# A two-layer token-mixing backbone: branch products among the attention units, pooling as a unit of its own, adaLN rows transposed one step later

## The chip, the cores and the metric

The kernel runs on one core of a Trainium2 chip. The metric is the device time of one execution in microseconds (us), as the median of several. The engines are called PE (matrix products), DVE (elementwise work), ACT (activations, casts, copies), POOL (elementwise work, slower) and SP (which here only issues DMA).

## What is computed

The reference is a network of two layers over 256 latent tokens and 256 context tokens, width 1024, in float32. Each layer is

```python
h = modulate(layer_norm(x), sh1, sc1)             # sh, sc, g: six rows of 1024 from silu(c) @ ada_w
mix = token_mixing(h, hc, lp, need_ctx)           # need_ctx only in the first layer
x = layer_norm(alpha * x + g1 * mix);  x = layer_norm(alpha * x + g2 * mlp(modulate(x, sh2, sc2)))
# token_mixing:
z, xbc, dt, qkv, pool, fnet, gate = split(h @ in_w + in_b)
y = g_ssd * (ssd(xbc, dt, z) @ ssd_out_w) + g_na * (attention(qkv) @ na_out_w) \
  + g_pool * (pool_branch(pool) @ pool_out_w) + g_fnet * (fourier(fnet) @ fnet_out_w)
mix = y @ mix_out_w                               # g = sigmoid(gate), four times 1024 columns
```

The pool branch takes centred window means (windows 2, 4, 8, 16) of the tokens in four groups of 192 columns, subtracts the token, and multiplies each group by a 192 x 192 matrix. The attention has 16 heads; the SSD has four groups. In the first layer all 512 tokens go through everything (`NX = 512`), in the second only the 256 latent tokens go on behind the mixers (`NX = 256`).

## The kernel before

Activations lie transposed, features on partitions and tokens along the row. Each float32 product is made of three products of rounded halves: `hi` is a rounded copy, `lo` the rest. A weight tile of 128 columns (`W`) is loaded by SP (512 KB), rounded by ACT to `whi` (L153) and subtracted by DVE to `wlo` (L154); there are three buffers. One product of a 1024-deep contraction is 24 matmuls (`mm3`, L186: `h_hi,whi`, `h_lo,whi`, `h_hi,wlo` for each of eight slices). An activation is split in the same way by `split_to` (L200 on ACT, L201 on DVE); in the profile these halves are `part`, or `plh` and `pll` in the pool.

A layer goes on like this. `first_products`, then `Driver.run` over thirteen units: `dt_unit`, and four times `ssd_unit` (group g) and two `attn_unit` (two heads each). A unit is a generator; where it yields, the driver puts in work that has come due. An SSD unit ends with squares summed on PE (L668), a power on POOL (L671), its spreading by PE (L675) and the scaled result `yt` on DVE (L679). An attention unit scores two heads (L719, L720 on PE), takes the softmax (DVE L729, L731, L733; ACT L734; DVE L735, L736; the context part is L745 to L754), transposes it on PE (L764, L772), copies it (ACT L765, L774) and multiplies by the values (L797, L802), which gives `oat` (L805).

Behind the units come the four branches in turn, each a `branch_unit` (L818): for each of eight output tiles a gate (24 matmuls from `h`, then ACT's tanh into `gth`, L816) and a branch product (from the split parts). Branch 0 (SSD) writes `mg` (L832), the others multiply and add (L834 on DVE, L835 on POOL). Each gate is emitted one tile ahead. Between branch 1 (attention) and branch 2 (pool) stands the pool stage in straight code: four `pool_tile`, `pool_map` 0, two `pool_tile`, two gates of branch 2, `pool_map` 1. A pool tile is a product of `h` (24 matmuls), window sums on DVE (`pwa`, `pwb`, L854), scaling (L872), subtraction (L874) and a split (`plh`, `pll`). A map is 21 matmuls over three split tiles with small weights (128 x 384), and writes the parts of branch 2 (L888, L889).

The adaLN rows (`ada_steps`) are made bit by bit between other work: a step multiplies 16 times (L295) into `adarows` (copied by ACT, L302), and `ada_flush` transposes them on PE (L315) for DVE to reduce (L317). Rows as they are needed for a gate are made by `rows_of` (L1027 on DVE, L1029 on PE, L1031 on DVE). At the start of the MLP, L370 transposes the normalised tokens, and DVE makes `h_hi` (L377) and `h_lo` (L378).

The order of an engine's instructions comes from a list scheduler: among those that are ready by its reckoning it takes the one emitted first, where weight loads and splits count as emitted 150 places earlier. So emission order is what the code decides, and each engine then works through its own list in order.

Of the kernel before, what the change touches and what calls it, by code (L numbers as in the profile page):

```python
# [10 lines left out]
F32R = mybir.dt.float32r  # L11
# [4 lines left out]
P = 128  # L16
D = 1024
KD = 8
# [11 lines left out]
NG = ((2,2),(2,2))  # L30
# [6 lines left out]
OFF = {256: 16, 512: 0}  # L37
# [36 lines left out]
def hybrid_backbone_kernel(ctx: ExitStack, tc: tile.TileContext, I, out, dbg=None):  # L74
# [21 lines left out]
    def T2(shape, name, dt=F32):  # L96
        return t2p.tile(shape, dt, tag="t2", name=name)
# [61 lines left out]
    def W(src, kt=KD, cols=P, scale=None, ahead=AHEAD, off=0):  # L159


        n = kt * cols
        hi = whl.tile([P, KD * P + 64], F32R, tag="hi", name="whi")[:, off:off + KD * P]
        lo = whl.tile([P, KD * P + 64], F32R, tag="lo", name="wlo")[:, off:off + KD * P]
        with tc.high_priority(offset=ahead):
            st = load_w(src, kt, cols)
            split_w(st[:, 0:n], n, hi[:, 0:n], lo[:, 0:n], scale)
        hi = hi[:, 0:n].rearrange("p (k c) -> p k c", c=cols)
        lo = lo[:, 0:n].rearrange("p (k c) -> p k c", c=cols)
        return lambda x, k: (hi, lo)[x][:, k, :]  # L170
# [111 lines left out]
    def ada_steps(l):  # L282


        steps = len(ADA_ORDER) // 2
        for n in range(steps):
            if (l, n) not in ready:
                ada_load(l, n)
            sts, ahead = ready.pop((l, n))
            ada_flush(l)  # L290
            pa = PS()
            for q in range(4):
                i, kc = q // 2, q % 2
                for k in range(4):
                    pe.matmul(pa[32 * k:32 * k + 32, 0:256], csil[:, 4 * kc + k, 2 - 2 * i:34 - 2 * i], sts[q](k),  # L295
                              start=(q == 0), stop=(q == 3), tile_position=(0, 32 * k))
            if not ahead:
                c = next(((l, m) for m in range(n + 1, steps) if (l, m) not in ready), (l + 1, 0))
                if c[0] < DEPTH:
                    ada_load(*c)  # L300
            rows = T2([P, 256], "adarows")
            act.copy(rows, pa[:, 0:256])  # L302
            open_[l] = (n, rows)
            yield

    open_, ready = {}, {}
    done = [0] * DEPTH

    def ada_flush(l):
        if l not in open_:  # L310
            return
        n, rows = open_.pop(l)
        pt = PS()
        for i in range(2):
            pe.transpose(pt[:, P * i:P * i + P], rows[:, P * i:P * i + P], ident)  # L315
        tmp = S([P, 2, 4], "adat")
        dve.tensor_reduce(tmp, pt[:, 0:256].rearrange("p (i c r) -> p i r c", i=2, c=4)[:, :, 0:4, :], axis=AX.X,  # L317
                          op=ALU.add)
        for j, g in enumerate(ADA_ORDER[2 * n:2 * n + 2]):
            o = _COLS["ada"] + 2 * g  # L320
            dve.tensor_tensor(mods[l][:, 2 * g:2 * g + 2, :], tmp[:, :, 2 * j:2 * j + 2],
                              colst[l][:, o:o + 2].unsqueeze(2).to_broadcast([P, 2, 2]), op=ALU.add)
# [65 lines left out]
    def layer(l, need_ctx, h, ws, load_x, final, prepare=None):  # L388

        NX = 512 if need_ctx else 256  # L390
# [3 lines left out]
        hx = NX / 512.0  # L394
# [111 lines left out]
        yt = {}  # L506
# [176 lines left out]
        oat = {}  # L683
# [128 lines left out]
        def gate(b, m):  # L812

            pg = inproj(M_GATE + 8 * b + m, NX)
            ths[b, m] = T2([P, 512], "gth")[:, 0:NX]
            act.activation(ths[b, m], pg[:, 0:NX], AF.Tanh, bias=col("gate", 8 * b + m), scale=0.5)  # L816

        def branch_unit(b, name, kt, a):  # L818
            if (b, 0) not in ths:
                gate(b, 0)  # L820
                yield "h", hx
            for m in range(KD):
                if m + 1 < KD and (b, m + 1) not in ths:
                    gate(b, m + 1)
                    yield "h", hx
                th = ths.pop((b, m))
                w = W(I[name][l, m], kt, off=OFF[NX])
                py = PM()
                mm3(py[:, 0:NX], w, a, K8[:kt], lambda t, k: t[k])
                if b == 0:  # L830
                    mg[m] = T2([P, 512], "mg")[:, 0:NX]
                    dve.scalar_tensor_tensor(mg[m], th, 1.0, py[:, 0:NX], op0=ALU.add, op1=ALU.mult)  # L832
                else:
                    dve.scalar_tensor_tensor(th, th, 1.0, py[:, 0:NX], op0=ALU.add, op1=ALU.mult)  # L834
                    pool.tensor_tensor(mg[m], mg[m], th, op=ALU.add)  # L835
                yield "h", hx
# [43 lines left out]
        def pool_map(pr_, pd, phl):  # L880
            ab = ([x[0] for x in pd], [x[1] for x in pd])
            for i in range(3):
                m = 3 * pr_ + i
                w = W(I["pool_w"][l, pr_, i], 3, off=OFF[NX])
                ks = [(k, k) for k in ((0, 1), (0, 1, 2), (1, 2))[i]]
                py = PS()
                mm3(py[:, 0:NX], w, ab, ks, lambda t, k: t[k][:, 0:NX])
                act.activation(phl[0][m], py[:, 0:NX], AF.Identity, scale=col("pscale", m))  # L888
                dve.scalar_tensor_tensor(phl[1][m], py[:, 0:NX], col("pscale", m), phl[0][m].bitcast(F32),  # L889
                                         op0=ALU.mult, op1=ALU.subtract)  # L890
# [81 lines left out]
                split_to(fhl[0][m], fhl[1][m], ft[:, 0:NS].rearrange("p s t -> p (s t)"))  # L972

        def parts(k=KD):
            return tuple([T2([P, 512], f"part{x}", F32R)[:, 0:NX] for _ in range(k)] for x in range(2))

        def split_tiles(src):
            a = parts()
            for m in range(KD):
                split_to(a[0][m], a[1][m], src.pop(m)[:, 0:NX])  # L980
            return a
# [3 lines left out]
        dr = Driver()  # L985
        units = [dt_unit(fp[0])]
        for g in range(4):
            units.append(ssd_unit(g, fp[1:] if g == 0 else None))
            units += [attn_unit(2 * g), attn_unit(2 * g + 1)]
        dr.run(units)  # L990
        if dbg:
            dbg("y", l, [yt[m][:, 0:NX] for m in range(KD)])
            dbg("o", l, [oat[m][:, 0:NX] for m in range(KD)])
        if need_ctx:
            layer_cols(l + 1)
        dr.run([branch_unit(0, "ssd_out_w", KD, split_tiles(yt))])
        dr.run([branch_unit(1, "na_out_w", KD, split_tiles(oat))])
        phl = parts(6)
        pds = [[], []]
        for i in range(3):  # L1000
            pool_tile(0, i, pds[0])
        pool_tile(1, 0, pds[1])
        pool_map(0, pds[0], phl)
        pool_tile(1, 1, pds[1])
        pool_tile(1, 2, pds[1])
        for m in range(NG[l][0]):
            gate(2, m)
        pool_map(1, pds[1], phl)
        dr.run([branch_unit(2, "pool_out_w", 6, phl)])
        fourier_load()  # L1010
        fhl = parts(6)
        fourier(fhl)
        dr.run([branch_unit(3, "fnet_out_w", 6, fhl)])


        mhl = parts()
# [150 lines left out]
        for c in range(4):  # L1167
            if c == 3:
                ada(l, 100)
                ada_flush(l)  # L1170
                if need_ctx:
                    ada(l + 1, 4, 4)
                    ada_flush(l + 1)
                g2 = rows_of(5)
            a2 = parts()
            m0 = 0
            if c == 0 and need_ctx:
                ws = ups
                m0 = len(ws)
                pls = [PM(), PM(), PM(), PS(), PS()][:m0]  # L1180
                for sl in (XS, CS):
                    for m in range(m0):
                        mm3(pls[m][:, sl], ws[m], h2, K8, lambda t, k: t[:, k, sl])
                for m in range(m0):
                    up_sink(pls[m], a2, c, m)
            for m in range(m0, KD):
                w = W(I["mlp_up_w"][l, 8 * c + m], off=48 if c == 1 else OFF[NX])
                ps = PM()
                mm3(ps[:, 0:NX], w, h2, K8, lambda t, k: t[:, k, 0:NX])
                up_sink(ps, a2, c, m)  # L1190
                if need_ctx:
                    ada(l + 1, 1, min(4, (8 * c + m) // 4 + 1))
            if c < 3:
                for n in range(2):
                    def sink(ps, t, n=n, c=c):
                        if c == 0:
                            acc[t, n] = T2([P, 512], "macc")
                            dve.tensor_tensor(acc[t, n], ps, db[n], op=ALU.add)
                        else:
                            dve.tensor_tensor(acc[t, n], acc[t, n], ps, op=ALU.add)  # L1200

                    half(lambda kk: I["mlp_down_w"][l, c, n, kk], a2, sink)
# [199 lines left out]
```

## Time and profile before

| | |
|---|---|
| median of 3 runs | 2121.72 us (2121.46 to 2122.72) |
| the profiled execution | 2120.56 us |
| its span | 2118.8 us |
| PE busy | 96% |
| DVE, ACT, POOL busy | 61%, 48%, 12% |
| bytes read from HBM | 293.75 MB |

The profiled execution is a single one, of which the hardware recorded the instructions; the span is from the first to the last instruction recorded. PE is busy almost throughout, so the profile is to be read for the short stretches in which it is not, one by one in the timeline, and for the clock that it was granted (1.00 is full speed).

### The profile page before, as it was taken

To read this page: it belongs to the slowest core of one execution; us is meant where nothing else is said; L and a number is where in the kernel's file an instruction comes from. 1 tells how busy PE (TensorE), PEld (TensorE's weight loads), DVE (VectorE), ACT (ScalarE), POOL (GpSimd) and SP (SyncE) were. 2 spreads that over 40 slices of the span, in tenths; PEclk is the share of its full clock that TensorE was granted. 3 is DMA by queue.
4 is the path that set the end of the run, shared out by engine and by line. 5 is a ranking of instruction groups with operands and counts; after the bars stand their busy time and mean duration, and the time that the engine had idled before them with its cause. 6 is when DMAs were issued, how large, how long until landed. Compare 5 with 4: busy or idle time off the path is not lost. (4 is left out here: it accounts for less than half of the span.)

```text
span 2118.8 us, 31149 instructions
## 1 busy us (share of the span) xinstructions
PE 2043.7 (96%) x12008; PEld 1703.3 (80%) x12008; DVE 1291.9 (61%) x2319; ACT 1019.9 (48%) x1787; POOL 247.6 (12%) x244
## 2 busy tenths in 40 slices
PE   6999999999999999999999999999999999998998
PEld 3777777777888888878888887877887898997997
DVE  4687686864336534475333357788778557566557
ACT  3576575763323323334232233576667545445443
POOL 0001000000001010112011111001000000112112
PEclk8999999999999999999999999999999999999999
DMA  7534243432332531335343333424345466566664
GB/s 287 172 130 161 98 160 100 159 105 81 99 100 82 181 107 54 99 120 179 117 151 92 98 120 120 172 83 150 109 131 165 122 193 207 184 208 210 190 193 142
DMA packets 94467, 298.16 MB, mean 141 GB/s; under 512 B 10928, under 2 KB 18800, under 8 KB 94320
## 3 DMA queue, kind: packets, MB, share of 16 engines
q1 hardware_dynamic: 94320, 296.19, 43.2%
q8 instruction: 94, 1.54, 0.3%
q14 instruction: 53, 0.43, 0.1%
HBM read 293.75 MB, written 2.39 MB: 140 GB/s over the span
## 5 line engine op out<-in xcount | busy, mean ns | idle before, releaser
L154 DVE TENSOR_TENSOR wlo<-st,whi 128x1024 fp32r<-128x1024 f32 (+3 forms) x382 | 477.0, 1250 | 453.2 <-ACT whi L153 434.4
L153 ACT CAST whi<-st 128x1024 fp32r<-128x1024 f32 (+3 forms) x382 | 386.2, 1012 | 713.0 <-PE pm L186 493.4
L186 PE MATMUL pm<-h_hi,whi 128*128 128x512 f32 (+1 forms) x1944 | 678.2, 349 | 3.3 <-DVE qb L698 1.3
L186 PE MATMUL pm<-h_lo,whi 128*128 128x512 f32 (+1 forms) x1944 | 674.0, 347 | 3.0 <-DVE h_lo L378 3.0
L186 PE MATMUL pm<-h_hi,wlo 128*128 128x512 f32 (+1 forms) x1944 | 673.5, 347 | 0.9 <-DVE wlo L154 0.9
L186 PEld LDWEIGHTS pm<-h_hi,whi 128*128 128x128 f32 x1944 | 367.0, 189 | 54.4 <-issue 6.1
L186 PEld LDWEIGHTS pm<-h_hi,wlo 128*128 128x128 f32 x1944 | 366.7, 189 | 50.2 <-issue 4.8
L186 PEld LDWEIGHTS pm<-h_lo,whi 128*128 128x128 f32 x1944 | 367.4, 189 | 49.1 <-DVE h_lo L378 3.2
L195 PE MATMUL pm<-whi,part 128*128 128x512 f32 x784 | 243.4, 390 | 0.1
L186 PE MATMUL pm<-part,whi 128*128 128x512 f32 (+1 forms) x896 | 218.8, 335 | 2.7 <-DVE part L201 1.1
L195 PEld LDWEIGHTS pm<-whi,part 128*128 128x128 f32 x784 | 146.5, 188 | 31.1 <-DVE part L1019 0.5
L186 PEld LDWEIGHTS pm<-part,whi 128*128 128x128 f32 x896 | 152.4, 188 | 22.3 <-DVE part L201 2.0
L195 PE MATMUL pm<-wlo,part 128*128 128x512 f32 x392 | 152.7, 389 | 0.0
L186 PE MATMUL pm<-part,wlo 128*128 128x512 f32 (+1 forms) x448 | 149.4, 334 | 0.5 <-DVE wlo L154 0.5
L1163 POOL TENSOR_TENSOR relu<-relu 128x512 f32<-128x512 f32 (+1 forms) x64 | 86.3, 1349 | 390.6 <-ACT relu L1160 387.0
L835 POOL TENSOR_TENSOR mg<-mg,gth 128x512 f32<-128x512 f32 (+1 forms) x48 | 55.3, 1152 | 525.0 <-DVE gth L834 348.2
L517 DVE SCALAR_TENSOR_TENSOR cacc<-cv,cols,cacc 128x512 f32<-128x512 f32 (+1 forms) x128 | 92.8, 725 | 8.2 <-ACT cacc L515 6.4
L186 PEld LDWEIGHTS pm<-part,wlo 128*128 128x128 f32 x448 | 84.1, 188 | 9.4 <-DVE wlo L154 0.7
L195 PEld LDWEIGHTS pm<-wlo,part 128*128 128x128 f32 x392 | 73.6, 188 | 15.2
L628 POOL TENSOR_TENSOR line<-line 128x512 f32<-128x512 f32 (+1 forms) x32 | 41.3, 1293 | 260.0 <-ACT line L624 219.4
L624 ACT ACTIVATE line<-line,nA 128x128 f32<-128x128 f32 x192 | 61.3, 395 | 12.1 <-DVE line L622 12.0
L834 DVE SCALAR_TENSOR_TENSOR gth<-gth,pm 128x512 f32<-128x512 f32 (+1 forms) x48 | 26.5, 552 | 63.6 <-PE pm L186 63.6
(260 smaller groups left out, 2540.7 us busy)
## 6 DMA issues: line engine op xcount, KB each, us to landing
st<-in_w SPq DMA_DIRECT2D x184, 512.0 KB, 3.6
ad<-ada_w SPq DMA_DIRECT2D x88, 512.0 KB, 6.0
st<-mlp_up_w SPq DMA_DIRECT2D x64, 512.0 KB, 3.6
st<-mlp_down_w SPq DMA_DIRECT2D x64, 512.0 KB, 3.6
bia<-rpb SPq DMA_DIRECT2D x16, 512.0 KB, 4.9
line<-sums SPq DMA_DIRECT2D x32, 256.0 KB, 6.7
st<-ssd_out_w SPq DMA_DIRECT2D x16, 512.0 KB, 3.6
st<-na_out_w SPq DMA_DIRECT2D x16, 512.0 KB, 3.6
```

Of the source, the lines that this page charges most:

```text
L153: act.copy(hi, st)
L154: dve.tensor_tensor(lo, st, hi.bitcast(F32), op=ALU.subtract)
L186: pe.matmul(ps, w(x, kw), rhs(a[y], ka), start=(i == 0 and j == 0), stop=(i == n - 1 and j == 2))
L195: pe.matmul(ps, a[y][k][:, P * t:P * t + P], w(x, i), start=(k == 0 and j == 0), stop=(k == KD - 1 and j == 2))
L517: dve.scalar_tensor_tensor(acc, c[:, 0:ns, k:k + 256], col("convw", 5 * m + k), acc, op0=ALU.mult, op1=ALU.add)
L624: act.activation(ex[:, t], ex[:, t], AF.Exp, bias=nAv[:, t, d, hd:hd + 1])
L628: pool.tensor_tensor(ed[0][:, 0:NT], ed[0][:, 0:NT], ed[1][:, 0:NT], op=ALU.add)
L834: dve.scalar_tensor_tensor(th, th, 1.0, py[:, 0:NX], op0=ALU.add, op1=ALU.mult)
L835: pool.tensor_tensor(mg[m], mg[m], th, op=ALU.add)
L1163: pool.tensor_tensor(r2, r, r, op=ALU.mult)
```

## The change

Four edits go together.

1. `ada_flush(l)` moves from ahead of a step's 16 matmuls to behind them: the rows of the step before are transposed later.
2. Branch 0 is handed to the driver as the last of the units, instead of in a run of its own. Its `split_tiles(yt)` is called when it gets to the first product; until all eight `yt` are there (`ready`), gates are emitted.
3. The pool stage becomes a unit, `pool_unit`, and runs with branch 1: behind it in the list in the first layer (`need_ctx`), ahead of it in the second, where each map is preceded by a yield `"w", 1` that lets branch 1 in.
4. `parts` puts two 256-column parts into one buffer; the weights of the MLP's second chunk get the same offset as the others (48 before).

```diff
             sts, ahead = ready.pop((l, n))
-            ada_flush(l)
             pa = PS()
...
                               start=(q == 0), stop=(q == 3), tile_position=(0, 32 * k))
+            ada_flush(l)
...
-        def branch_unit(b, name, kt, a):
+        def branch_unit(b, name, kt, a, ready=lambda: True):
...
+                if m == 0:
+                    for n in range(2, KD):
+                        if not ready():
+                            gate(b, n)
+                            yield "h", hx
+                    a = a()
...
-            return tuple([T2([P, 512], f"part{x}", F32R)[:, 0:NX] for _ in range(k)] for x in range(2))
+            n = 512 // NX
+            ts = [[T2([P, 512], f"part{x}", F32R) for _ in range(k // n)] for x in range(2)]
+            return tuple([ts[x][i // n][:, NX * (i % n):NX * (i % n) + NX] for i in range(k)] for x in range(2))
...
+        phl = []
+        def pool_unit():
+            phl.extend(parts(6))
+            pds = [[], []]
+            for i in range(3):
+                pool_tile(0, i, pds[0])
+                yield "h", hx
+            pool_tile(1, 0, pds[1])
+            yield "h", hx
+            if not need_ctx:
+                yield "w", 1
+            pool_map(0, pds[0], phl)
+            pool_tile(1, 1, pds[1])
+            yield "h", hx
+            pool_tile(1, 2, pds[1])
+            yield "h", hx
+            if need_ctx:
+                for m in range(NG[l][0]):
+                    gate(2, m)
+            else:
+                yield "w", 1
+            pool_map(1, pds[1], phl)
+        dr.run(units + [branch_unit(0, "ssd_out_w", KD, lambda: split_tiles(yt), lambda: len(yt) == KD)])
...
-        dr.run([branch_unit(0, "ssd_out_w", KD, split_tiles(yt))])
-        dr.run([branch_unit(1, "na_out_w", KD, split_tiles(oat))])
...
+        b1 = branch_unit(1, "na_out_w", KD, lambda: split_tiles(oat))
+        dr.run([b1, pool_unit()] if need_ctx else [pool_unit(), b1])
+        dr.run([branch_unit(2, "pool_out_w", 6, lambda: phl)])
...
-                w = W(I["mlp_up_w"][l, 8 * c + m], off=48 if c == 1 else OFF[NX])
+                w = W(I["mlp_up_w"][l, 8 * c + m], off=OFF[NX])
```

In the rows below, a `...` stands where rows are left out. Line numbers of the changed kernel are 1 to 20 off behind the changed places (L839 to L896 are L832 to L889 of before, L1051 is L1031).

PE at the end of layer 1's mixers, before: from the last score product of the last head (L720) through its softmax's transposes (L764) to branch 0's first product (`part`).

```order
L720 MATMUL psx<-kk_4244,qb_4101 128x256
L186 MATMUL pm<-h_hi,whi 128x512
...
L764 MATMUL psx<-cons,sc 128x128 x2
L186 MATMUL pm<-h_hi,whi 128x512
...
L764 MATMUL psx<-cons,sc 128x128 x6
L772 MATMUL psx<-cons,scc 128x128 x4
L797 MATMUL psx<-PT,vk 64x256 x8
L802 MATMUL psx<-PC,vk 64x256 x4
...
L186 MATMUL pm<-part_4672,whi 128x512
```

The same place after the change, from the transposes of the last but one head.

```order
L764 MATMUL psx<-cons,sc 128x128 x8
L772 MATMUL psx<-cons,scc 128x128 x4
...
L719 MATMUL psx<-kk_4244,qa_4099 128x256
L720 MATMUL psx<-kk_4244,qb_4101 128x256
L764 MATMUL psx<-cons,sc 128x128 x8
L186 MATMUL pm<-part_4695,whi 128x512
L772 MATMUL psx<-cons,scc 128x128 x4
L186 MATMUL pm<-h_hi,whi 128x512
L186 MATMUL pm<-part_4703,whi 128x512
```

The products of `h` that stood behind the last scores are gone from there, and the first branch product has come up between the last head's L764 and L772.

PE at the end of layer 2's mixers, before, from the last two score products.

```order
L719 MATMUL psx<-kk_14135,qa_14063 128x512
L720 MATMUL psx<-kk_14135,qb_14065 128x512
L186 MATMUL pm<-h_lo,whi 128x256
...
L764 MATMUL psx<-cons,sc 128x128 x2
L797 MATMUL psx<-PT,vk 64x256
L764 MATMUL psx<-cons,sc 128x128 x6
L797 MATMUL psx<-PT,vk 64x256 x7
L186 MATMUL pm<-part_14468,whi 128x256
```

The same place now.

```order
L719 MATMUL psx<-kk_14135,qa_14063 128x512
L720 MATMUL psx<-kk_14135,qb_14065 128x512
L675 MATMUL psx<-cons,rs 128x128 x2
L764 MATMUL psx<-cons,sc 128x128 x2
L797 MATMUL psx<-PT,vk 64x256
L186 MATMUL pm<-part_14543,whi 128x256 x2
L764 MATMUL psx<-cons,sc 128x128
L186 MATMUL pm<-part_14547,whi 128x256
```

Here too the products of `h` (17 before) have left the place behind the scores, L675 of the last SSD group has come there, and branch 0's products begin between the two heads' transposes.

DVE in layer 2, before: `part<-oat` are the halves for branch 1's products, `pwa` and `pll` the first and last step of the pool's tiles.

```order
L832 SCALAR_TENSOR_TENSOR mg<-gth,pm 128x256
L154 TENSOR_TENSOR wlo<-st,whi 128x1024
L201 TENSOR_TENSOR part_15036<-oat,part_15028 128x256
...
L201 TENSOR_TENSOR part_15043<-oat,part_15035 128x256
L834 SCALAR_TENSOR_TENSOR gth<-gth,pm 128x256
...
L854 TENSOR_TENSOR pwa<-pu 128x270
...
L201 TENSOR_TENSOR pll<-pl,plh 128x256
```

DVE in layer 2 after the change, at the end of the pool's tiles.

```order
L881 TENSOR_TENSOR pl<-pl,pu 128x256
L896 SCALAR_TENSOR_TENSOR part_15024<-psx,cols,part_15021 128x256
L201 TENSOR_TENSOR pll<-pl,plh 128x256
L201 TENSOR_TENSOR part_15438<-oat,part_15434 128x256 x2
L201 TENSOR_TENSOR part_15439<-oat,part_15435 128x256 x2
L201 TENSOR_TENSOR part_15440<-oat,part_15436 128x256 x2
L201 TENSOR_TENSOR part_15441<-oat,part_15437 128x256 x2
L841 SCALAR_TENSOR_TENSOR gth<-gth,pm 128x256
```

The halves for branch 1 stood ahead of the whole pool; they now stand behind its last `pll`.

DVE at the start of layer 2's MLP, before.

```order
L1072 TENSOR_SCALAR xn<-xt,lnsum 128x1024
L377 CAST h_hi<-htmp 128x2x256
L378 TENSOR_TENSOR h_lo<-htmp,h_hi 128x2x256
L377 CAST h_hi<-htmp 128x2x256
L378 TENSOR_TENSOR h_lo<-htmp,h_hi 128x2x256
```

The same place now; `grow` is the copy of a gate's rows out of PSUM.

```order
L1092 TENSOR_SCALAR xn<-xt,lnsum 128x1024
L377 CAST h_hi<-htmp 128x2x256
L1051 COPY grow<-psx 16x128
L378 TENSOR_TENSOR h_lo<-htmp,h_hi 128x2x256
L377 CAST h_hi<-htmp 128x2x256
L378 TENSOR_TENSOR h_lo<-htmp,h_hi 128x2x256
```

The copy of the gate's rows has moved in between the first `h_hi` and the first `h_lo`.

## Rows read from the trace of the kernel before

**Rows 1.** Profile page: busy time of each engine, its share of the span, instructions.

```profile
PE 2043.7 (96%) x12008; PEld 1703.3 (80%) x12008; DVE 1291.9 (61%) x2319; ACT 1019.9 (48%) x1787; POOL 247.6 (12%) x244
```

**Rows 2.** PE's waits over the run: who, for what; us, times, longest.

```profile
PE psx L764 <- DVE sc L736: 8.2, 10, 1.1
...
PE psx L295 <- ACT PC L774: 1.1, 1, 1.1
```

**Rows 3.** Timeline of PE, end of layer 1's mixers: start, length, instruction, wait before.

```profile
465.16 2.07 PE L675 MATMUL psx<-cons,rs 128*128 128x128 f32 x8 [0.77 <-POOL rs L671]
...
475.84 0.40 PE L186 MATMUL pm<-h_hi,whi 128*128 128x512 f32 x1
...
490.07 0.51 PE L186 MATMUL pm<-part,whi 128*128 128x512 f32 x1 [0.62 <-DVE part L201]
```

**Rows 4.** The same view of DVE and ACT, the last head's softmax in layer 1.

```profile
475.10 0.42 DVE L729 CUSTOM_DVE_ANT_0 sc<-psx,bia 128x256 f32<-128x256 f32 x1 [1.28 <-PE psx L720]
...
477.95 0.48 DVE L736 TENSOR_SCALAR sc<-sc,mx 128x512 f32<-128x512 f32 x1
...
480.08 0.20 ACT L750 ACTIVATION_READ_ACCUMULATOR scc<-psx,mxc 128x1 f32 x1
```

**Rows 5.** Windows: length, PE busy (matmuls), mean granted clock, DMA share, GB/s.

```profile
464.00:469.00 5.00, 4.23 (x19) 0.66 0.93 312
1441.00:1449.00 8.00, 7.51 (x36) 0.57 0.43 132
1664.00:1672.00 8.00, 4.73 (x30) 1.00 0.33 111
1690.00:1710.00 20.00, 20.00 (x179) 1.00 0.65 200
1799.00:1819.00 20.00, 20.00 (x172) 1.00 0.77 249
1150.00:1170.00 20.00, 20.00 (x90) 1.00 0.27 89
```

**Rows 6.** Timeline of PE, end of layer 2's mixers.

```profile
1658.31 0.71 PE L675 MATMUL psx<-cons,rs 128*128 128x128 f32 x4 [0.34 <-POOL rs L671]
...
1662.44 0.28 PE L186 MATMUL pm<-h_lo,whi 128*128 128x256 f32 x1
...
1664.27 0.28 PE L186 MATMUL pm<-h_hi,wlo 128*128 128x256 f32 x1
1665.66 0.41 PE L764 MATMUL psx<-cons,sc 128*128 128x128 f32 x2 [1.12 <-DVE sc L736]
...
1667.64 0.87 PE L764 MATMUL psx<-cons,sc 128*128 128x128 f32 x6 [0.99 <-DVE sc L736]
1668.87 1.94 PE L797 MATMUL psx<-PT,vk 128*64 128x256 f32 x14 [0.35 <-ACT PT L765]
1671.57 0.84 PE L186 MATMUL pm<-part,whi 128*128 128x256 f32 x2 [0.77 <-ACT part L200]
```

**Rows 7.** Timeline of DVE there, the last head's softmax in layer 2.

```profile
1662.18 0.42 DVE L729 CUSTOM_DVE_ANT_0 sc<-psx,bia 128x256 f32<-128x256 f32 x1
...
1665.03 0.49 DVE L736 TENSOR_SCALAR sc<-sc,mx 128x512 f32<-128x512 f32 x1
```

**Rows 8.** Layer 2's pool stage: windows of PE and DVE, and DVE's timeline.

```profile
1754.39:1789.50 35.11, 31.23 (x254) 1.00 0.58 183
...
1754.39:1789.50 35.11, 28.51 (x55) 1.00 0.58 183
...
1759.42 0.43 DVE L854 TENSOR_TENSOR pwa<-pu 128x270 f32<-128x270 f32 x1
...
1785.72 0.42 DVE L201 TENSOR_TENSOR pll<-pl,plh 128x256 fp32r<-128x256 f32 x1 [0.47 <-ACT plh L200]
```

**Rows 9.** Timeline of PE and DVE, start of layer 2's MLP.

```profile
1927.14 3.46 PE L370 MATMUL psx<-cons,xn 128*128 128x128 f32 x15 [0.30 <-DVE xn L1072]
...
1929.59 0.69 DVE L378 TENSOR_TENSOR h_lo<-htmp,h_hi 128x512 fp32r<-128x512 f32 x1
```

More of the change, by code (lines that the diff above doesn't have):

```diff
@@ L989, in layer @@
             units += [attn_unit(2 * g), attn_unit(2 * g + 1)]
[L990 to L993, printed above, removed]
+        phl = []
[21 more added lines that the diff above has]
+        dr.run(units + [branch_unit(0, "ssd_out_w", KD, lambda: split_tiles(yt), lambda: len(yt) == KD)])
         if need_ctx:
             layer_cols(l + 1)
-        dr.run([branch_unit(0, "ssd_out_w", KD, split_tiles(yt))])
-        dr.run([branch_unit(1, "na_out_w", KD, split_tiles(oat))])
[L998 to L1009, printed above, removed]
+        b1 = branch_unit(1, "na_out_w", KD, lambda: split_tiles(oat))
+        dr.run([b1, pool_unit()] if need_ctx else [pool_unit(), b1])
+        dr.run([branch_unit(2, "pool_out_w", 6, lambda: phl)])
         fourier_load()
@@ L1012, in layer @@
         fourier(fhl)
-        dr.run([branch_unit(3, "fnet_out_w", 6, fhl)])
+        dr.run([branch_unit(3, "fnet_out_w", 6, lambda: fhl)])
         mhl = parts()
```

## The prediction, made before the changed kernel had run

> **What bounds the kernel now.** I read the page first: TensorE (PE) is busy for 96% of the span, VectorE (DVE) for 61% [rows 1]. So only a pause of PE, a slower clock of PE or a slower step from one matmul to the next is worth time. Next the table of PE's waits, which says what is left: its longest group over the run is the attention transposes (L764) waiting for the softmax's last scaling (L736), ten times, 8.2 us, none over 1.1; another is L295 waiting once, 1.1, for a copy of ACT [rows 2]. Then the timelines of the places that the change touches, which give each wait its moment, and windows for the clock. In the rows below a wait in brackets stands behind the instruction that waited. The loss is a little more than the bracket, because the matmuls no longer overlap: the product at 1664.27 would have been followed 0.11 later, at 1664.38; the next starts at 1665.66 [rows 6], which is 1.28 for a bracket of 1.12. I add 0.2 to 0.3 to a bracket.
>
> **The change part by part**, as gain or loss of PE time.
>
> (a) adaLN rows one step later. Over the run nothing is computed twice or left out; the transposes L315 go behind the sixteen L295 of the next step. The one place where this changes what PE waits for is early in layer 1, where L295 stood behind L315 and waited 1.1 [rows 2]: that goes if the copy is ready 2 us later. Elsewhere the transposes stand between products that cover them. +1.1, bounds 0 and +1.1.
>
> (b) Branch 0 among the last units of layer 1. What goes: the wait of L675 for the normalisation on GpSimd (0.77) and that of the first branch product for its split on DVE (0.62) [rows 3], with the overlap 1.7. [...] The change puts a gate's 24 products ahead of L675, so that L668's result has 5.4 us to come back (24 at 0.227, since 20 us hold about 88 of this layer's [rows 5]), and I let the fall go too. Together +3.4.
>
> What comes: the order rows show that the change emits three gates of branch 0 early, and uses them up one head sooner. Before, the last head's scores were followed by 12 and then 8 products. Now the eight L764 follow the last L720 directly. PE is done with the scores when the next product starts, at 475.84; the softmax runs L729 from 475.10 to the end of L736 at 477.95 + 0.48 = 478.43 [rows 3, 4]. That is a chain of DVE and ACT which no weight work lengthens, so PE would wait 478.43 − 475.84 = 2.6. Behind it, the first branch product needs the hi cast of `yt`, which ACT does after the softmax's last read (480.08 [rows 4]), and then DVE's lo half: two hand-overs, each by the like wait at 490.07 (0.62) about 0.7. Sum 4.0. So −0.6 for (b); it would be +2.6 if each stop cost no more than 0.8 in all, and −2.9 if the clock didn't recover either and the hand-overs took 1.0.
>
> (c) The same in layer 2. What goes are five brackets, 0.34, 1.12, 0.99, 0.35 and 0.77 [rows 6], 3.57, with the overlap 5.0. What comes: the 17 products between the last L720 and the first L764 are no longer there, only two L675. The chain from L729 (1662.18) to the end of L736 (1665.03 + 0.49 = 1665.52) [rows 7] is the same, the first L764 comes about where it did, and PE, free at 1662.44 [rows 6] plus 0.4 for the two L675, stands for 2.9. After that 46 branch products cover the second half of the softmax and the copies; 0.5 for what is left over. +1.6; bounds −2.0 (the split of `yt` waits behind the softmax on ACT as well) and +4.2 (all new waits 0.8).
>
> (d) Pooling as a unit of branch 1, layer 2. In layer 1 the order stays branch 1, then pool. In layer 2 it turns round: branch 0, pool, branch 1. Before, the pool stage runs from 1754.39 to 1789.50; 254 matmuls in 35.11 us [rows 8] at 0.1133 (the step of the layer: 20 us hold about 176.5 of the 179 counted, whose first and last overlap the edges [rows 5]) are 28.8, so 6.3 are lost there. The reason is DVE: from the first window sum (1759.42) to the last lo split (1785.72 + 0.42 = 1786.14) its work is 26.7 long [rows 8], starting 5.0 after the first tile's product. Now, on the order rows of DVE, all eight lo splits of `oat`, which branch 1's first product needs, stand behind the last `pll`; so that product can't start before 5.0 + 26.7 + 0.5 for a weight split more + 0.4 for the first `oat` split = 32.6 after the first tile. What PE has to do until then: four tiles and two gates (144), the first map (21), two tiles (48), two thirds of the second (13): 226 × 0.1133 = 25.6. 7.0 are lost against 6.3: −0.7. The products of branch 1, which are many enough to cover the pool, come too late to do it. Bounds −3.5 (the buffers of the small weights held by waiting products) and +4 (DVE, 19% idle in that stage with 28.51 busy of 35.11 [rows 8], closes its own gaps).
>
> (e) A side effect at the start of the MLP of layer 2. The rows of the gate (`rows_of`, L1029 on PE, L1031 on DVE) move early; L1031 now stands on DVE between the first `h_hi` and the first `h_lo`, and waits for L1029, which stands behind the 16 transposes L370. These end at 1927.14 + 3.46 = 1930.60; L378 started at 1929.59 [rows 9]. So `h_lo` comes 1.0 later, and with it the second matmul, which is `h_lo,whi`. −1.0, bounds −1.2 and 0.
>
> The offset of the weights in the MLP's second chunk, and half as many buffers for the parts, move no wait that I can find: 0.
>
> **Sum**: 1.1 − 0.6 + 1.6 − 0.7 − 1.0 = +0.4. The profiled execution took 2120.56, so 2120.2; the median of three stands 1.2 higher, so 2121.3. That is no change: about 0.2% (4.2 us) is what a measurement of this kernel can tell from none, so faster begins below 2117.5 and slower above 2126.0.
>
> **The rivals.** (1) The new waits are as short as the old: no stop of L764 over 1.1 has been seen in ten [rows 2], and if the softmax of the last heads meets other covers than I read from the order, each stop costs 0.8. Then (b) is +2.6, (c) +4.2, the sum 6.2, the time 2115.5. It makes the kernel faster from the point where the added waits are 3.5 together instead of 7.4. For it: DVE is free of weight splits there. Against: the chain of rows 4 has only steps that stay.
>
> [...]
>
> (3) The step. In layer 2 the products run at one of two steps: 179 begun or running in 20 us in the first branches, 172 in the third [rows 5], 0.1133 and 0.1178 each. The slow one is there behind the pool stage. If now it is there in branches 0 and 1, some 670 products take 4.4 ns more each: 3.0, time 2124.3. If it goes from branch 2 (480 products) it is +2.1: 2119.2. Neither decides.
>
> **How the numbers follow.** Forecast 0.47, rival 1 0.26, rival 2 0.16, rival 3 0.11. The forecast's own range by the bounds is 2117 to 2126; 0.03 of its chance I give to each side beyond 0.2%. Faster 0.26 + 0.03 = 0.29, slower 0.16 + 0.03 = 0.19, same 0.52. The range is 2114.5 to 2127.0: it reaches past rival 1's time and up to where one stretch at the lower clock and a worse hand-over lead; outside lie the rest of rival 2 and a tenth below.
>
> **What the changed profile would show.** (a) No wait of L295 for L774. (b) After the last L720 of layer 1 a wait of L764 for L736 of 2 to 2.6, none of L675, granted clock 1.00 around L675. (c) The same of 2.5 to 2.9 in layer 2, then no wait up to the branch products. (d) Branch 1's first product waiting for a lo split of `oat`, some 32 us after the first pool tile. (e) `h_lo` 1 us after `h_hi`. The forecast is wrong if L764's waits are under 1 (rival 1), if a window after one of them shows 0.6 (rival 2), or if DVE's chain in the pool stage is shorter than 24 us.

## The result and the profile after

The changed kernel takes 2134.52 us (median of 4 runs, 2133.01 to 2136.68), the kernel before 2121.59 beside it: a ratio of 1.0063, 95% interval 1.0051 to 1.0075. It is 13 us slower, where no change was forecast, and lies above the range. The profiled execution took 2135.57, its span is 2133.8 us, 15.0 longer than before. The first line of the page of after shows what the first group of before showed [rows 1], and it doesn't show the loss: PE's share is the same 96%, since PE is also busy while it runs at half clock (484 to 486: busy throughout at a granted clock of 0.50).

```profile
PE 2054.7 (96%) x12008; PEld 1712.8 (80%) x12008; DVE 1290.7 (60%) x2319; ACT 1018.4 (48%) x1787; POOL 249.1 (12%) x244
```

To find the place, the start of the same instruction was read in both traces. The last column is how much later it comes after the change; where that figure grows, time is lost.

```
instruction (number of before)                     before     after     later
L719, an attention unit late in layer 1            441.29    441.16     -0.13
L832, fourth product of branch 0, layer 1          526.23    527.40     +1.18
L834, second product of branch 1, layer 1          591.50    596.60     +5.10
L834, second product of branch 2, layer 1          718.93    723.19     +4.26
L1160, first tile of layer 1's MLP                 971.24    976.39     +5.15
L719, an attention unit late in layer 2           1625.16   1628.60     +3.44
L832, last product of branch 0, layer 2           1710.33   1716.51     +6.18
L834, third product of branch 2, layer 2          1800.22   1813.75    +13.54
L1046, start of the mixing's normalisation        1902.70   1916.47    +13.77
L1160, first tile of layer 2's MLP                1935.89   1951.97    +16.07
L1063, end of the program                         2113.77   2128.78    +15.01
```

Four steps make up the loss: the mixers' end of layer 1 (+1.3), branch 1 of layer 1 (+3.9), layer 2 from the mixers' end to branch 2 (+10.1), and the stretch from the mixing's normalisation to layer 2's MLP (+2.3). That is 17.6 together; other stretches give 2.6 back. PE's waits in the two stretches that the forecast had treated, layer 1's last head and layer 2's, stand in one table each (who waited, for whom: us in total, times, longest). The first row is that of the last head in layer 1, the second that of layer 2, to be read with [rows 3, 6]. The `gcol` of the first is a small copy that DVE ended right behind the softmax's last scaling (L736); the table names what ended last.

```profile
PE psx L764 <- DVE gcol L1047: 2.7, 1, 2.7
...
PE psx L764 <- DVE sc L736: 3.3, 1, 3.3
```

At 576, between branch 0 and branch 1 of layer 1, is a wait that before doesn't have: the first product of branch 1 waits for a cast of ACT. ACT's timeline says why. The casts of the attention output stand behind the second gate's tanh (L816); that tanh needs the gate's product, and it stands behind a weight cast that waited 3.80 for PE itself.

```profile
PE pm L186 <- ACT part L200: 2.0, 1, 2.0
...
576.13 1.04 ACT L153 CAST whi<-st 128x1024 fp32r<-128x1024 f32 x1 [3.80 <-PE pm L186]
577.08 0.68 ACT L816 ACTIVATE gth<-pm,cols 128x512 f32<-128x512 f32 x1
577.66 1.65 ACT L200 CAST part<-oat 128x512 fp32r<-128x512 f32 x3
```

In before the same casts were done while branch 1's first gate ran on PE, well ahead of branch 1's first product:

```profile
565.04 3.74 ACT L200 CAST part<-oat 128x512 fp32r<-128x512 f32 x7
```

The waits of PE in layer 2's pool stage, after the change, add up to 6.8; in the stage of before [rows 8] the same list adds up to 3.8. All rows below but one (1.4) are waits for weights.

```profile
PE psx L186 <- ACT whi L153: 2.7, 2, 2.3
PE psx L186 <- DVE wlo L154: 1.7, 1, 1.7
PE psx L186 <- ACT plh L200: 1.4, 1, 1.4
PE pm L186 <- DVE wlo L154: 0.6, 1, 0.6
PE pm L186 <- ACT whi L153: 0.4, 1, 0.4
```

Last the windows of after (length, PE busy and matmuls, granted clock, DMA share, GB/s), to be read with [rows 5]. The first four are the two tails, the new stop at 576 and the pool stage, and in each of them the clock falls. In both traces it stands at 1.00 or at 0.50, so 8 us at 0.79 are 3.4 us at 0.50, and 16 us at 0.68 are 10.2. At 0.50 layer 2's products start 0.21 to 0.23 apart (1752.57 to 1753.87), against 0.1178 at 1.00 (1716.31 to 1720.43). The last two are the steps of layer 2's products in the first and third branch: both are slow now, where before only the third was.

```profile
480.00:488.00 8.00, 5.13 (x23) 0.79 0.22 69
576.00:584.00 8.00, 6.00 (x20) 0.79 0.21 66
1672.00:1680.00 8.00, 5.61 (x31) 0.79 0.23 68
1744.00:1760.00 16.00, 11.72 (x63) 0.68 0.74 236
1690.00:1710.00 20.00, 20.00 (x172) 1.00 0.54 176
1800.00:1820.00 20.00, 20.00 (x172) 1.00 0.58 183
```

Added up over all matmuls of the two traces, from one start to the next, the 15.0 us are some 2 to 3 more of standing still, 9 to 10 more of products at half clock and 3.2 more of the slower step. The split is an estimate, from the distance of neighbouring starts to 0.2267 (512 columns) and 0.1133 (256 columns); a stop that falls into the lower clock can be counted either way. It says that a stop cost more than its length.

### The profile page after: what moved, and what is told of

It is laid out like the page before. It is cut to its first block, busy times and chain, and to the rows that moved or that the text cites. A ratio compares the mean times of both kernels' runs of the same rounds, so it can differ in the third digit from the quotient of the medians.

```text
span 2133.8 us, 31144 instructions
## 1 busy us (share of the span) xinstructions
PE 2054.7 (96%) x12008; PEld 1712.8 (80%) x12008; DVE 1290.7 (60%) x2319; ACT 1018.4 (48%) x1787; POOL 249.1 (12%) x244
## 5 line engine op out<-in xcount | busy, mean ns | idle before, releaser
L186 PE MATMUL pm<-part,whi 128*128 128x512 f32 (+1 forms) x896 | 224.0, 340 | 2.1 <-ACT part L200 2.0
```

The source lines that it names most:

```text
L186: pe.matmul(ps, w(x, kw), rhs(a[y], ka), start=(i == 0 and j == 0), stop=(i == n - 1 and j == 2))
```

## Experiments

The theory after this reading: three things cost, each through PE standing still and what comes behind a stop. They are the late split of the attention output in layer 1, the pool of layer 2 ahead of branch 1 with the split behind it, and the shared buffers. The rival: it is the merged branch 0, or the stops' cost is only moved. Ratios below are to the kernel before beside them on the same chip; a hundredth of a per cent is 0.2 us.

### The split of the attention output put back, layer 1

The changed kernel with:

```diff
-        b1 = branch_unit(1, "na_out_w", KD, lambda: split_tiles(oat))
+        sp1 = [split_tiles(oat)] if need_ctx else []
+        b1 = branch_unit(1, "na_out_w", KD, lambda: sp1[0] if sp1 else split_tiles(oat))
```

> The changed kernel, with one line put back: in layer 1 the eight halves of the attention output are split before branch 1's first two gates are emitted, not behind them. Theory (the late split): in the changed kernel the casts stand on ACT behind the second gate's tanh and PE stands still for 2.2 us at 576, after which the granted clock is 0.5 for 3.4 us (1.7 of work). Both go, so about 3.9 us less than the changed kernel: 2130.6 against 2134.5. Rival (the loss there is only moved: the buffers of the parts are not free earlier, or the clock falls elsewhere): no change, 2134.5, within 1 us.

2129.73 us, ratio 1.0042 (1.0025 to 1.0059) against 1.0063: 4.5 us less, though the intervals overlap. The trace decides: the wait at 576 and the fall of the clock behind it are gone, and so is the step of 3.9 us in branch 1. ACT's timeline has the last of the casts ahead of the first tanh again:

```profile
570.40 0.61 ACT L200 CAST part<-oat 128x512 fp32r<-128x512 f32 x1
570.92 0.68 ACT L816 ACTIVATE gth<-pm,cols 128x512 f32<-128x512 f32 x1
```

So this line of the diff, `a = a()` behind the gates instead of an argument worked out ahead of the run, costs about a third of the loss.

### Branch 0 among the units, alone

The kernel before with `branch_unit` as in the change, and:

```diff
-        dr.run(units)
...
-        dr.run([branch_unit(0, "ssd_out_w", KD, split_tiles(yt))])
-        dr.run([branch_unit(1, "na_out_w", KD, split_tiles(oat))])
+        dr.run(units + [branch_unit(0, "ssd_out_w", KD, lambda: split_tiles(yt), lambda: len(yt) == KD)])
+        sp1 = split_tiles(oat)
+        dr.run([branch_unit(1, "na_out_w", KD, lambda: sp1)])
```

> The kernel before, with only branch 0 emitted among the last units. Theory (every new stop costs its length and a stretch of 3.4 us at the lower clock behind it, 1.7, and in layer 2 the products behind it run at the slower step): layer 1 +1.3, layer 2's tail +1 to +2 and the step of some 700 products 4.4 ns slower, +3: together 2126 to 2128. Rival (the tails are even, as forecast, and the loss is in the pool): 2121.0 to 2122, the step 0.1133 in branches 0 and 1.

2123.98 us, ratio 1.0010 (1.0001 to 1.0019): 2.1 us slower, between the two expectations. The windows show which half of the theory held. The stops are there (5.12 and 4.75 busy of 8), but in this profile the clock stayed at 1.00 behind both; the step is the slow one in branches 0 and 1.

```profile
480.00:488.00 8.00, 5.12 (x30) 1.00 0.22 69
1666.00:1674.00 8.00, 4.75 (x34) 1.00 0.39 133
1690.00:1710.00 20.00, 20.00 (x172) 1.00 0.60 187
1725.00:1745.00 20.00, 20.00 (x173) 1.00 0.61 192
1800.00:1820.00 20.00, 20.00 (x179) 1.00 0.75 259
```

In this profile, the tails by themselves come out even, as forecast: layer 1's later branches stand at 0.0 to +0.3 against before. Layer 2 loses 2.6 from the third product of branch 0 (+1.0) to the end of branch 1 (+3.6), which some 600 products at 4.4 ns more account for. The profiled execution, 2121.65, is the second fastest of ten, which go up to 2126.62; seven of them had a mean granted clock of 0.987 to 0.990, against its 0.991. So that no fall stands behind the stops is shown for this execution alone.

### The pool of layer 2 as a unit, alone

The kernel before, with `branch_unit` and, in layer 2 alone, `pool_unit` as in the change, and

```diff
+            dr.run([pool_unit(), branch_unit(1, "na_out_w", KD, lambda: split_tiles(oat))])
```

> The kernel before, with only the pool stage of layer 2 as a unit ahead of branch 1, whose split is emitted when it gets to its first product. Theory (the pool chain on DVE is uncovered, and a stretch of 6.8 to 10.2 us at the lower clock follows): pauses of 10 us in the stage instead of 7, and 3 of clock: 2121.6 + 6 = 2127 to 2129. Rival (the pool as a unit is even, as forecast, -0.7, and the loss needs the merged branch 0 ahead of it): 2121.5 to 2123.

2127.68 us, ratio 1.0031 (1.0017 to 1.0045): 6.6 us slower. PE's waits in the stage add to 6.0, and the clock falls there without any merged branch ahead of it (16 us at 0.79 are 6.8 at 0.50). The rival is out: the pool needs nothing else to cost.

```profile
PE psx L186 <- ACT plh L200: 2.2, 1, 2.2
PE psx L186 <- DVE wlo L154: 1.6, 1, 1.6
PE psx L186 <- ACT whi L153: 1.0, 2, 0.6
...
1740.00:1756.00 16.00, 12.07 (x69) 0.79 0.76 257
```

### The same with the split ahead of the pool

```diff
-            dr.run([pool_unit(), branch_unit(1, "na_out_w", KD, lambda: split_tiles(oat))])
+            sp1 = split_tiles(oat)
+            dr.run([pool_unit(), branch_unit(1, "na_out_w", KD, lambda: sp1)])
```

> The pool unit of layer 2 alone, as in the run of that (e3), but with the eight splits of the attention output emitted ahead of the pool. Theory (branch 1's products can't cover the pool because their own splits stand behind it on DVE and ACT; the second map's pauses, 1.8 and 2.5 us, are PE standing between the maps with nothing else to do): branch 1's products move in ahead of the second map, the pauses there fall from 8 us to 3 or 4, and the stretch at the lower clock goes: 2127.7 - 6 = 2121 to 2123. Rival (the pool standing ahead of branch 1 is what costs, the split's place in the list nothing): 2126 to 2128, the same pauses.

2121.23 us, ratio 0.9998 (0.9989 to 1.0007): no different from before, 7.0 us less than with the late split. A product of branch 1 and a gate now stand on PE between the last tiles and the second map. The waits of the stage are 2.8 together, and the clock is at 1.00 in the same 16 us.

```profile
PE psx L186 <- ACT plh L200: 1.7, 2, 1.2
PE pm L186 <- DVE wlo L154: 0.8, 2, 0.5
PE psx L186 <- DVE pll L201: 0.3, 1, 0.3
...
1738.00:1754.00 16.00, 13.56 (x107) 1.00 0.81 268
```

So it isn't the pool's place ahead of branch 1 that costs, but eight splits behind the pool's chain on DVE and ACT, which keep branch 1's products from covering that chain.

### The adaLN edit alone

The kernel before with `ada_flush(l)` behind the step's matmuls.

> The kernel before, with only the adaLN rows transposed one step later. Theory (even but for the wait of 1.1 in layer 1): 2120.5, within 1 us of before. Rival (it moves the three steps at the start of layer 2's MLP and layer 1's, where the changed kernel is 2.3 and 0.9 later): 2124 to 2125.

2118.69 us, ratio 0.9989 (0.9980 to 0.9999): faster, by 0.2 to 4.2 us. In the profiles the first layer's units gain 0.9 from 54 to 441 us, as the forecast's 1.1; another 1.4 is the clock's in this execution, which at 1441 was low for half as long as the 6.8 us of before (0.57 from 1441 to 1449 [rows 5]). The rival's 2 to 3 us of loss isn't there.

### Buffers of their own for the parts

The changed kernel with `parts` as it was.

```diff
-            n = 512 // NX
-            ts = [[T2([P, 512], f"part{x}", F32R) for _ in range(k // n)] for x in range(2)]
-            return tuple([ts[x][i // n][:, NX * (i % n):NX * (i % n) + NX] for i in range(k)] for x in range(2))
+            return tuple([T2([P, 512], f"part{x}", F32R)[:, 0:NX] for _ in range(k)] for x in range(2))
```

> The changed kernel with each 256-column part in a buffer of its own again, as before. Theory (the shared parts leave buffers free, so that the adaLN loads of layer 2's MLP and the load behind the last mixing weights go out in another order; PE's wait of 2.7 us for the wq cast at 1922 and part of what follows come from there): that wait is gone, 2 to 3 us less than the changed kernel's 2134.5: 2132. Rival (that wait comes from the one-step-later transposes or from the pool's order): the wait stays, 2134 to 2135.

2130.07 us, ratio 1.0047 (1.0026 to 1.0068) against 1.0063: 3.4 us less, though the intervals overlap. The traces decide: the changed kernel has this wait in layer 2's mixing, ahead of the MLP, which the run with buffers of their own (and before) doesn't have. Part of it comes back, because the wait for the normalisation that follows (L370, the second row) is shorter than with buffers of their own (the third):

```profile
PE pm L195 <- ACT wq L153: 2.6, 1, 2.6
...
PE psx L370 <- ACT xn L1094: 2.5, 1, 2.5
...
PE psx L370 <- ACT xn L1092: 4.4, 1, 4.4
```

Of all thirteen profiles here, the four of kernels that share all parts (the changed one twice, the run with the early split in layer 1, and the run below with the tiles between) have the `wq` wait, 2.0 to 2.6, and come 2.0 to 2.5 later from the mixing's normalisation to the MLP's first tile than before; the other nine have no such wait and come at most 0.6 earlier.

SP's queue shows where it comes from (start, length, issue). In the changed kernel six of the mixing's loads go out ahead of `gd`, the write of a gate's rows, and the last mixing load, which `wq` is cast from, stands behind `gd`, its reading back (`gb`) and eight adaLN loads:

```profile
1894.28 12.98 SPq L147 DMA_DIRECT2D st<-mix_out_w  x6
1908.46 0.33 SPq L1053 DMA_DIRECT2D gd<-grow  x1
1909.59 0.34 SPq L147 DMA_DIRECT2D st<-mix_out_w  x1
1911.60 0.80 SPq L1060 DMA_DIRECT2D gb<-gd  x2
1912.45 5.26 SPq L274 DMA_DIRECT2D adh<-ada_w  x8
1918.02 0.33 SPq L147 DMA_DIRECT2D st<-mix_out_w  x1
```

With buffers of their own `gd` goes out behind five loads, as in before, and the last one 21.7 us after the first instead of 23.7:

```profile
1889.30 10.25 SPq L147 DMA_DIRECT2D st<-mix_out_w  x5
1900.08 0.33 SPq L1051 DMA_DIRECT2D gd<-grow  x1
...
1911.02 0.33 SPq L147 DMA_DIRECT2D st<-mix_out_w  x1
```

Why free buffers shift that write is an argument from the scheduler's rule (what has a buffer is taken by emission order) and wasn't shown.

### Both kernels once more

> The changed kernel once more, for a second profile. Theory (pauses are the program's, but which of them is followed by a stretch at the lower clock, and which step the products of layer 2 take, differs from one execution to the next): the same waits within 0.3 us each, other stretches in two or more places, 2131 to 2136. Rival (the stretches belong to the program too): the same stretches at the same places, 2133.5 to 2135.5.

> The kernel before once more, for a second profile: by the theory the same waits, other stretches at the lower clock or another step in some of the four places in which layer 2's products ran at 0.1133 or 0.1178, 2118 to 2125; by the rival the same of both, 2121 to 2122.

2132.1 and 2121.45 us, one execution each. From 50 us up to the start of layer 2's MLP PE's pauses are the same within 0.4 us each, except five in the changed kernel and two in before that differ by 0.5 to 1.1 (one of them in the pool stage of each kernel: 1.39 instead of 2.42, and 0.61 instead of 1.51); at the MLP's start they differ by up to 1 us. The stretches at the lower clock are partly the same. In the changed kernel, 480 to 488, 576 to 584 and 1672 to 1680 have 0.79 again; but layer 1's MLP, at 0.65 in the first profile, is at 1.00 in the second, and the pool stage has 6.8 us of it instead of 10.2:

```profile
952.00:960.00 8.00, 4.94 (x34) 1.00 0.48 160
...
1744.00:1760.00 16.00, 13.21 (x77) 0.79 0.87 295
```

The step is the same in both profiles of each kernel, in every place looked at (172 and 172 of the changed one, 179 and 173 of before). So the theory was half right: stretches differ in part between executions, the step belongs to the program.

### The pool's tiles between branch 1's products

The kernel before with the adaLN edit and the shared parts; in layer 2 (16 yields of branch 1: two gates, then product and gate in turn):

```diff
+            sp1 = split_tiles(oat)
...
+            for _ in b1:
+                n += 1
+                if n in (3, 5, 7, 9, 11, 12, 13):
+                    steps[(3, 5, 7, 9, 11, 12, 13).index(n)]()     # six tiles, map 0 as the fifth
+            gate(2, 0)
+            pool_map(1, pds[1], phl)
```

> The kernel before with the adaLN edit and the shared parts, and in layer 2 the pool's six tiles and first map emitted one by one between branch 1's products, the splits of the attention output ahead of them, the second map behind branch 1. Theory (what costs in the pool is that DVE's chain has no products of branch 1 beside it): the pauses of the stage, 6 to 7 us before and 10 in the changed kernel, fall below 2, nothing falls in clock there: 2118.7 (the adaLN edit alone) - 5 = 2114. Rival (the small weights of the maps share the three weight buffers, so PE waits for them wherever the maps stand): pauses of 5 and more at the two maps, 2118 to 2120.

2121.97 us, ratio 1.0003 (0.9990 to 1.0016): inconclusive in time, clear in the trace. The chain of the pool's tiles on DVE no longer holds PE anywhere. One wait of 2.8 stands behind the second map, for the next gate's weights:

```profile
PE pm L186 <- ACT whi L153: 2.8, 1, 2.8
PE pm L186 <- DVE wlo L154: 1.2, 2, 0.8
```

A map's three products are over in some 2.4 us and take all three weight buffers, so the rival is right for what follows a map. In this profile, what stands against the gain is the wait for `wq` (2.4, the shared buffers again), 3.4 us at the lower clock from 1784, behind the wait of 2.8, and a stretch at 0.53 from 1664 to 1675, a place that this edit doesn't touch.

### The maps' products apart

The same, each of the six small products between others, and buffers shared only for the split attention output and the maps' results:

```diff
+            steps = {3: (0, 0), 5: (0, 1), 7: (0, 2), 9: (1, 0), 10: 0, 12: (1, 1), 13: 1, 14: (1, 2), 15: 2}
+            for n, _ in enumerate(b1, 1):
+                v = steps.get(n)
+                if isinstance(v, tuple):
+                    pool_tile(*v, pds[v[0]])
+                elif v is not None:
+                    pool_map(0, pds[0], phl, (v,))
+            for m in range(3):
+                gate(2, m)
+                pool_map(1, pds[1], phl, (m,))
```

> The kernel before with the adaLN edit; in layer 2 the six pool tiles between branch 1's products, and each of the six small products of the two maps between other products too, so that their three weight buffers aren't taken by three short products in a row; shared buffers only for the split attention output and for the maps' results. Theory (the pauses of the stage are DVE's chain uncovered, and behind a map the next weights coming late, 3.0 and 0.9 us in the run with the tiles between): pauses in the stage under 1.5 us against 6.3 before, the wq wait gone too: 2118.7 - 5 = 2114. Rival (the small weights come late wherever they stand): 2117 to 2119.

2113.2 us, ratio 0.9964 (0.9950 to 0.9977): 7.6 us faster than before, some 21 faster than the changed kernel. All that PE waits for in the stage is

```profile
PE pm L186 <- DVE wlo L154: 0.6, 1, 0.6
PE pm L186 <- DVE part L895: 0.3, 1, 0.3
```

The adaLN edit, which is in this kernel too, gave 2.4 by itself. So most of the 6.3 that the pool stage cost was there to be had, with the tiles covered by products that have their own inputs ready.

### What is left of the change without the three

The changed kernel with the split of the attention output ahead of branch 1's gates in layer 1 and ahead of the pool in layer 2, and a buffer of its own for each part.

> The changed kernel with three things put back together: the split of the attention output ahead of branch 1's gates in layer 1, ahead of the pool in layer 2, and a buffer of its own for each part. What is left of the change is the adaLN edit, branch 0 among the units, the pool as a unit. Theory (these three are the whole loss, and add up): before 2121.3, adaLN alone -2.8, branch 0 alone +2.4, pool with early splits 0: 2120 to 2122. Rival (branch 0 among the units and the pool together cost more than each alone): 2124 and above.

2122.61 us beside 2123.16, ratio 0.9991 (0.9981 to 1.0002). From 1.0063 that is 15.3 us, and the three alone gave 4.5, 3.4 and 7.0 (1.0031 to 0.9998): 14.9. Each of the three alone is known to some 4 us only; together they are the whole loss, and what stays in (the adaLN edit, branch 0 among the units, the pool's place, the weights' offset) comes out even within the interval.

This kernel still has both tails with a fall of the clock in each:

```profile
480.00:488.00 8.00, 5.70 (x24) 0.79 0.23 69
1668.00:1676.00 8.00, 5.94 (x33) 0.79 0.18 60
```

So those two stretches by themselves don't make the kernel slower than before, which had a fall of its own at 464 [rows 5]: they are still there when the loss is gone.

## Why the prediction was wrong

**The step that failed first is a line that was read past.** The split of the attention output moved in both layers. In (d) the prediction followed it on DVE in layer 2; in layer 1 it said that "the order stays branch 1, then pool" and left it there. But `a()` is called behind the gates, and ACT's list, which the prediction shows nowhere for this place, has the casts behind a tanh that waits for PE. Its cost, 4.5 us by the run that puts it back, has no term in the sum.

**(d), the pool of layer 2: the order right, the size wrong.** Branch 1's first product came when its halves did, at 1752.57 behind the whole chain, 36.3 after the first tile's (1716.31); forecast were 32.6. PE's stops up to there stand at the products of the second map and of a tile ahead of it. The forecast had taken the chain as the 26.7 us of before with one split more. But DVE stands idle in it for weights whose casts come late, and one of these casts (the last row, on ACT) waits 2.35 for the load of its weight:

```profile
1740.34 1.23 DVE L154 TENSOR_TENSOR wlo<-st,whi 128x1024 fp32r<-128x1024 f32 x1 [0.99 <-ACT whi L153]
...
1744.11 1.22 DVE L154 TENSOR_TENSOR wlo<-st,whi 128x1024 fp32r<-128x1024 f32 x1 [1.72 <-ACT whi L153]
...
1743.03 1.46 ACT L153 CAST whi<-st 128x1024 fp32r<-128x1024 f32 x2 [2.35 <-DMA st<-in_w]
```

36.3 less 226 products at the step that they had, 0.1178, are 9.7 instead of 7.0; of the 3.0 that the lower clock costs in the stage, 1.2 lie in these 9.7 and 1.8 behind them. The term was −0.7; the pool alone measured −6.6, and with the split ahead of it nothing. The lower bound of −3.5 held no fall of the clock.

**The term set at 0 for the shared buffers** is −3.4 by the times and −2.0 to −2.5 by the traces of that place. The prediction found no wait that they move; one came in the mixing of layer 2, through SP's queue, of which it shows no row.

**(b) and (c) were nearly right as pauses and wrong as times.** Layer 1's new stops are 2.83 and 0.42 beyond the step from start to start, 3.3 against 4.0 forecast. Layer 2's are 3.47 and, at full clock in the run of branch 0 alone, some 0.35 behind it, 3.8 against 3.4: the chain from L729 to L736 takes about as long as forecast (3.2 against 3.3) but starts at 1671.03, behind a weight split of DVE, and L675 has four matmuls there instead of two. But the +3.4 in (b) counts 1.7 for a fall of the clock that was to go. No run shows that 1.7 as time; it is an estimate, half of the 3.4 us for which before has 0.50 from 464.8 on (0.66 from 464 to 469 [rows 5]). After the change a fall of the same 3.4 us stands at 483, and (c)'s stop brought one that wasn't there before, at 1674. Alone, branch 0 costs 2.1, where (b) + (c) gave +1.0; the slow step, 2.6 in that run's profile, is most of the difference.

**(a)** was right, 1.1 forecast; the edit alone gains 0.2 to 4.2. **(e)**, −1.0, was seen rightly and is the shared buffers' too: the copy stands between the first `h_hi` and `h_lo` in the four profiles with all parts shared and in none of the others. In the changed kernel `h_lo` starts 1.7 behind the start of `h_hi`, where before it was 0.5, and PE's list has 0.3 for it; the stage's loss is mostly the `wq` wait.

**The rivals.** Rival 2, the clock falling behind the two tails' stops, had the sign but not the places: it falls behind both (0.79 from 480 to 488 and from 1672 to 1680), but the kernel with the three things undone has both falls and is no slower than before. The falls that went with the loss stand behind the two stops that the prediction hadn't seen or had undersized, the longest of the four (10.2) in the pool stage. The profile of branch 0 alone has the two stops of the tails with the clock at 1.00, and the one with buffers of their own has layer 2's, 3.47 again, with none behind it; so a stop doesn't fix a fall by itself. Nor does the program fix every place of one: in the two profiles of the changed kernel the stretch in layer 1's MLP is present in one (0.65 from 952 to 960) and absent in the other (1.00). Rival 3, given as one that doesn't decide, came true together with it: the slow step stands in branches 0 and 1 of layer 2 and costs 3.2 by the starts, 3.0 forecast. Treating the rivals as either-or was itself a mistake: the stops, the falls and the step added.

What stays open: what sets the step of a place. It isn't a fall of the clock behind a stop (the profile of branch 0 alone has the slow step and no such fall in layer 2's tail), and it isn't one edit's: branch 0 alone moves it, and so does the adaLN edit alone (172, 179, as below). Why some stops are followed by a fall and others not is open too.

## What to carry to other kernels

Where a unit takes its input as something to be called, look at where the call lands in every engine's list, not in the code: a split that is emitted two gates later ran on the same engine two gates later, and cost PE a stop that nothing in its own list showed. Here a chain of small steps on one engine was covered only by products whose own inputs didn't stand behind it on that engine; put those inputs first, and short products that use up the weight buffers apart. Price a new stop of PE at its length and, as a bound, at a stretch of lower clock behind it (here 3.4 us at 0.50 behind three stops and 10.2 in the pool stage), and let such costs add instead of choosing between them.

## What was not expected of the hardware

The step of layer 2's products, 0.1133 or 0.1178 us at full clock, is the program's: the same in two profiles of each kernel, but moved between places by edits that don't touch those products. With the adaLN edit alone, branch 0 is slow, branches 1 and 2 are fast:

```profile
1690.00:1710.00 20.00, 20.00 (x172) 1.00 0.58 190
1727.00:1745.00 18.00, 18.00 (x162) 1.00 0.64 198
1800.00:1820.00 20.00, 20.00 (x179) 1.00 0.77 261
```

In the slow stretches about one weight load in three lasts 192 ns (56 of the 170 that start from 1690 to 1710 in the changed kernel), where nearly all last 187 or 188 in the fast ones (all 176 there in before); the matmuls' own order and tiles are the same in each place compared. What lengthens those loads isn't shown.
